# Sparse attention's key projections ahead of head three's gates; the stacking loop ordered head by head

## The chip, the cores and the metric

The kernel runs on one core of a Trainium2 chip. The metric is the device time of one execution in microseconds (us), here the median of three runs. The engines are named as in the profile: PE is TensorE (matmuls and transposes; PEld its weight loads), DVE is VectorE, ACT is ScalarE, POOL is GpSimd, and SP starts the DMAs.

## What is computed

One layer of a decoder trunk over 1024 tokens of width 1024. The normed input is projected once, and the columns of the result go to three groups of heads: a gated linear recurrence (group A, HGRN2, 4 heads of 128), sparse attention with an indexer that picks 256 keys for each query (group B, 4 heads of 64), and attention into 256 memory tokens (group C). Their outputs are joined and projected, and a SwiGLU layer follows. The change touches groups A and B:

```python
def hgrn2_mix(q, f_logit, i, g, lb, out_gain):
    ...
    def step(S, inp):
        qc, kc, vc, gc = inp
        b = jnp.cumsum(gc, axis=2)
        o_inter = jnp.einsum('bhck,bhkv->bhcv', qc * jnp.exp(b), S)
        diff = b[:, :, :, None, :] - b[:, :, None, :, :]
        decay = jnp.exp(jnp.where(causal[:, :, None], diff, -jnp.inf))
        A = jnp.einsum('bhtk,bhtsk,bhsk->bhts', qc, decay, kc)
        o = o_inter + jnp.einsum('bhts,bhsv->bhtv', A, vc)
        ...
        return S, o
    ...
    o = rmsnorm(o, out_gain) * jax.nn.silu(g.astype(f32))

def dsa_mix(q, k, v, iq, ik, iw, q_gain, k_gain):
    ...
    q = rmsnorm(q, q_gain).astype(f32)
    k = rmsnorm(k, k_gain).astype(f32)
    ...
        logits = jnp.einsum('bqhd,bqkhd->bhqk', qb, kg) * (SA_DH ** -0.5)
        logits = jnp.where(valid[:, None], logits, -jnp.inf)
        p = jax.nn.softmax(logits, axis=-1)
        return jnp.einsum('bhqk,bqkhd->bqhd', p, vg)
```

## The kernel before

**Stages.** In the order of time: norm of the input, indexer scores, memory attention, the projections of groups A and B with the recurrences between them, sparse attention (560 to 640 us), the output projection (`wo`), the SwiGLU layer (`ff`, `fo`). The change lies in the projections between 424 us and sparse attention.

**A projection.** `proj` (L186) takes one page of 128 columns of the weights and makes it in two halves `hf` of 512 tokens. A half is 24 matmuls of 128x512: each operand is split into a high and a low part, and three products of them are summed over eight tiles of the model width. The moving operand is the normed input, held in 32 tiles `ht(p, k, hf)` (p the part, k the width tile, hf the half); the result stands in one of two PSUM banks "mm" until `evac` has taken it out. Each page comes by one DMA (`hg_wst`, `sap_wst`) and is split on ACT (L117) and POOL or DVE (L118).

**Group A**, for each head h: `hgrn_proj(h)`, three pages; `hgrn_gates(h)`, sigmoids and products in POOL and ACT; `hgrn_intra(h)`, the products inside a block of 32 tokens in six rounds. A round is `level_products` (32 small matmuls on L518, printed in halves or whole) and then `descend` on the tiles Q, K and F, on DVE (L527), POOL (L528) and DVE (L529), and L543 which takes the round's products out. The next round's matmuls read the tiles that `descend` has just changed, so the rounds wait for one another: PE to DVE and POOL and back. Two wider rounds (L553) follow. `hgrn_state(h)` transposes K (L571), makes the products of keys and values (L578), chains them over the blocks on DVE (L583, L585), makes the output (L594, L596), squares and sums it (L601, L602), takes the inverse root (`narrow_rstd`, L144 to L151, fifteen DVE steps one behind the other) and applies it (L606, L612, L613).

**Group B.** `sparse_queries` projects page 20 and page 21 is projected last of all (`evac_q1`); `sparse_keys` projects pages 18 and 19, and for each half copies the keys into `mt(4)` or `mt(5)` (ACT L734; printed as `sap_m4`, `sap_m5`), squares them (L736), sums the squares (PE L739), takes the inverse root on DVE (L159, L144 to L151), spreads it over rows (L169 on DVE, L172 on PE) and multiplies the keys by it (L744). The storage of `mt(4)` holds the second head's values before. Then the **stacking loop** writes, for each of the four heads and both halves, the queries (`stack`, L253 and L254) and the keys into operand tiles: on ACT the high part (L810), on DVE or POOL the low part (L811). These operand tiles are `ht` tiles again: they lie over the normed input, so a tile of half hf can be written only when the last projection's half hf has read it. The stacked keys `kst` and queries `qst` are what sparse attention's logits read.

**Sparse attention** is a pipeline over 32 items (8 blocks of queries, 4 heads): `sa_logits` (PE L830, DVE L832 adds the mask and takes the maximum, L837 scales it by the query's norm), `sa_exp` (ACT L841), `sa_scale` (POOL L847), `sa_turn` (PE transposes L856, copies L859 on ACT and L861 on DVE), `sa_out` (PE L875). With each item one step of `fillers` is written: first the steps of `hgrn_intra(3)` and `hgrn_state(3)`, then parts of the output projection.

**What sets the order.** Each engine takes its instructions in one fixed order. It is not the order of the program text: a list scheduler places the whole program against a model of the engines' time, and of the instructions that are ready on an engine in that model the one that stands earliest in the text goes first. So moving a call in the text changes which work fills which gap, on all engines.

The calls between the second head's state and sparse attention read (`run` finishes all steps of a generator):

```python
    run(hgrn_state(1))
    hgrn_gates(2)
    run(hgrn_intra(2))
    hgrn_proj(3)
    hgrn_gates(3)
    sparse_keys()
    bisect((7, 4), V, "v")
    run(hgrn_state(2))
```

Heads are numbered from 0 in the code; "head three" in the text is `h = 2`, "head four" is `h = 3`. `bisect` is part of the indexer and finds each query's threshold.

## Time and profile before

| | before |
|---|---|
| median of 3 runs | 1390.32 us (1389.21 to 1392.29) |
| the profiled execution's own time | 1390.27 us |
| its span in the profile | 1388.5 us |
| mean granted clock of PE | 0.973 |
| PE busy | 1302.4 us (94%) |
| DVE busy | 1056.7 us (76%) |
| ACT busy | 692.0 us (50%) |
| POOL busy | 475.1 us (34%) |
| PE's share of the chain that ended last | 59% |
| DVE's share of it | 6% |

The busy times and shares come from the profile's page. The shares are means over stages that are limited in different ways, so they don't say what a change in one stage is worth. The page also cuts the span into 40 slices of 34.7 us and gives each engine's busy share in tenths; in slices 15 and 16 (from 520 to 590 us) PE stands at 5 and 7 (9 in most others), PE's granted clock at 6 and 8, and DVE at 9 and 7. That stretch is the one behind the last projection and ahead of sparse attention.

### The profile page before, as it was taken

The page shows a single profiled execution, that of the slowest core. Times are in us where ns is not written, and L with a number is a line of the kernel's source. Part 1 is how long each engine was busy: PE and PEld are TensorE (multiplying, and loading weights), DVE is VectorE, ACT ScalarE, POOL GpSimd, SP SyncE. Part 2 cuts the span into 40 slices and gives each one's busy share as a digit, 9 for nine tenths or more (in the row PEclk, how much of TensorE's full clock was granted, in tenths as well). Part 3 has the DMA queues.
Part 4 walks back from the last instruction along what each step waited for, and adds up shares of the span by engine and source line. Part 5 has one row for each costly group of instructions (what it writes and reads, how often), then busy time and mean ns, then how long its engine had stood idle before and what let it go on. Part 6 is the DMA issues. An engine that isn't in the chain of part 4 may idle for free.

```text
span 1388.5 us, 22035 instructions
## 1 busy us (share of the span) xinstructions
PE 1302.4 (94%) x8072; PEld 1066.3 (77%) x8072; DVE 1056.7 (76%) x2094; ACT 692.0 (50%) x1369; POOL 475.1 (34%) x395
## 2 busy tenths in 40 slices
...
DMA packets 53244, 122.19 MB, mean 88 GB/s; under 512 B 6032, under 2 KB 6160, under 8 KB 53136
## 3 DMA queue, kind: packets, MB, share of 16 engines
...
## 4 chain that ended last, share of the span: by engine, by line
PE 59%; DVE 6%; POOL 2%; ACT 2%; issue 2%; DMA 1%; ACTq 0%; DVEq 0%; POOLq 0%
PE ff_lg L1093 17%; PE ff_rc L1093 12%; PE fo_mm L1252 4%; PE fo_sm L1252 4%; PE wo_mm L1052 3%; PE fo_lg L1252 2%; PE fo_rc L1252 2%; PE wo_sm L1052 2%; PE sap_mm L186 2%; PE hg_mm L186 2%; PE sat_sm L856 1%; PE sat_lg L830 1%; PE wo_mm L186 1%; PE sat_mm L875 1%; PE sat_rc L875 1%
## 5 line engine op out<-in xcount | busy, mean ns | idle before, releaser
L117 ACT ACTIVATE ff_whi<-ff_x 128x512 fp32r<-128x512 f32 x112 | 70.0, 629 | 125.4 <-PE ff_rc L1093 70.1
L643 ACT ACTIVATE idx_x<-idx_x,packs 128x896 int8<-128x896 f32 (+3 forms) x128 | 105.7, 826 | 41.6 <-DVE packs L638 34.9
L1093 PE MATMUL ff_lg<-wo_h,ff_whi 128*128 128x512 f32 x396 | 104.8, 391 | 2.8 <-ACT wo_h L117 2.8
L186 PE MATMUL hg_mm<-xn_h,hg_whi 128*128 128x512 f32 x384 | 96.9, 395 | 0.0
L1093 PE MATMUL ff_rc<-wo_h,ff_whi 128*128 128x512 f32 x308 | 90.5, 393 | 0.6 <-DVE wo_h L177 0.6
L1093 PE MATMUL ff_lg<-wo_x,ff_whi 128*128 128x512 f32 x308 | 84.9, 404 | 5.3 <-ACT ff_tmp L1100 4.8
L1093 PEld LDWEIGHTS ff_lg<-wo_h,ff_whi 128*128 128x128 f32 x396 | 74.6, 188 | 18.7 <-ACT wo_h L117 3.3
L118 DVE TENSOR_TENSOR ff_wlo<-ff_x,ff_whi 128x512 fp32r<-128x512 f32 x112 | 82.1, 741 | 8.7 <-ACT ff_whi L117 4.0
L186 PEld LDWEIGHTS hg_mm<-xn_h,hg_whi 128*128 128x128 f32 x384 | 70.5, 188 | 14.5 <-issue 0.7
L118 POOL TENSOR_TENSOR hg_wlo<-hg_wst,hg_whi 128x512 fp32r<-128x512 f32 x32 | 43.0, 1356 | 104.9 <-ACT hg_whi L117 79.4
L1093 PEld LDWEIGHTS ff_lg<-wo_x,ff_whi 128*128 128x128 f32 x308 | 57.6, 192 | 24.0 <-ACT ff_whi L117 7.3
L646 DVE TENSOR_SCALAR_CACHE_REDUCE idx_x<-idx_x,packs 128x1024 int8<-128x1024 f32 x64 | 68.7, 1074 | 0.9
L1093 PEld LDWEIGHTS ff_rc<-wo_h,ff_whi 128*128 128x128 f32 x308 | 58.6, 190 | 13.6 <-DVE wo_h L177 1.4
L1093 PE MATMUL ff_rc<-wo_x,ff_whi 128*128 128x512 f32 x220 | 64.3, 389 | 0.0
L1030 POOL TENSOR_TENSOR ff_x<-ff_wst 128x512 f32<-128x512 f32 x7 | 13.4, 1911 | 134.6 <-PE wo_sm L1052 71.3
L528 POOL TENSOR_TENSOR hg_x<-hg_x,hg_x 128x256 f32<-128x256 f32 x56 | 49.4, 898 | 29.0 <-PE hg_rc L518 18.7
L1093 PE MATMUL ff_lg<-wo_h,ff_wlo 128*128 128x512 f32 x198 | 55.8, 390 | 0.0
L388 DVE SCALAR_TENSOR_TENSOR idx_x<-idx_tmp,packs,idx_x 128x512 f32<-128x512 f32 (+2 forms) x70 | 46.1, 710 | 12.2 <-ACT idx_tmp L383 11.9
L118 DVE TENSOR_TENSOR fo_wlo<-fo_tmp,fo_whi 128x512 fp32r<-128x512 f32 x33 | 33.2, 1006 | 27.0 <-ACT fo_whi L117 27.0
L186 PE MATMUL hg_mm<-xn_h,hg_wlo 128*128 128x512 f32 x192 | 50.9, 397 | 0.0
L1093 PEld LDWEIGHTS ff_rc<-wo_x,ff_whi 128*128 128x128 f32 x220 | 41.3, 188 | 8.6
L118 DVE TENSOR_TENSOR fo_wlo<-fo_h,fo_whi 128x512 fp32r<-128x512 f32 x31 | 33.5, 1081 | 18.1 <-ACT fo_whi L117 18.0
...
## 6 DMA issues: line engine op xcount, KB each, us to landing
...
```

The costliest lines, as they stand in the source:

```text
L117: S.activation(hi, src, AF.Copy)
L118: (eng or V).tensor_sub(lo, src, hi.bitcast(F32))
L186: T.matmul(ps[:M, :], w(pw, k), h[p][k][hf], start=i == 0, stop=i == len(order) - 1)
L388: V.scalar_tensor_tensor(sc[b][:, c0:c1], rl[:, :c1 - c0], iww[:, b, h:h + 1], sc[b][:, c0:c1], op0=ALU.mult, op1=ALU.add)
L528: G.tensor_mul(Kv[:, :, 0, :], Kv[:, :, 0, :], fr.to_broadcast([128, n, w]))
L643: S.activation(waste[S][:, :nk], sc[b], AF.Sign, bias=nf[:, j:j + 1], accum_out=ct[:, j:j + 1])
L646: eng.tensor_scalar(waste[eng][:, :nk], sc[b], fl[:, j:j + 1], None, op0=ALU.is_ge, op1=ALU.add, accum_out=ct[:, j:j + 1])
L830: T.matmul(lg[:, :c1 - c0], qst[h][b // 4][:, bs(b % 4)], kst[h][p][c][:, :c1 - c0], start=p == 0, stop=p == 1)
L875: T.matmul(po[ROWS[j], 0:128], sv[kb // 4][:, kb % 4, 128 * m + 64 * j:128 * m + 64 * j + 64], PTs[j][:, kb, :], start=kb == 0, stop=kb == ...
L1052: mm = T.matmul(ps, lhs, rhs, start=i == 0, stop=i == len(steps) - 1)
L1093: mm = T.matmul(ps, w[pw][:, bs(k)], HB[u][k][p], start=first and i == 0, stop=i == 11, skip_group_check=True)
L1252: T.matmul(banks[m], w[i][pw][:, bs(m)], b[i][p], start=first and i == 0 and n == 0, stop=i == NP - 1 and n == 2, skip_group_check=True)
```

## The change

The call of `sparse_keys()` moves from behind head four's gates to a place ahead of head three's gates, so that the key projections come ahead of head three's rounds and of head four's projections. The stacking loop runs over the heads outside and the halves inside; before, it ran over the halves outside and the heads inside. The operations in both loops are the same ones, and each engine issues as many of them as before.

```diff
@@ -775,11 +775,11 @@
     run(hgrn_intra(1))
     hgrn_v(1)
     run(hgrn_state(1))
+    sparse_keys()
     hgrn_gates(2)
     run(hgrn_intra(2))
     hgrn_proj(3)
     hgrn_gates(3)
-    sparse_keys()
     bisect((7, 4), V, "v")
     run(hgrn_state(2))
     bisect((6, 5, 3, 2), S, "s")
@@ -796,19 +796,18 @@
     ph[0] = "sap"
     proj(page(21), 128, H, evac_q1)
     kst = [[[None, None], [None, None]] for _ in range(4)]
-    for hf in range(2):
-        for m in range(2):
-            for j in range(2):
-                h = 2 * m + j
-                if m == 0:
-                    qst[h][hf] = ht(0, h, hf)
-                    stack(qst[h][hf].unsqueeze(1), sqr[0][:, hs(hf)], 0, ROWS[j], V_SAQ)
-                for p in range(2):
-                    kst[h][p][hf] = ht(1 - p, h + 4 * p, hf)
-                src = kr[m][ROWS[j], hs(hf)]
-                for o, e in ((ROWS[j], V), (ROWS[1 - j], G)):
-                    S.activation(kst[h][0][hf][o], src, AF.Copy)
-                    e.tensor_sub(kst[h][1][hf][o], src, kst[h][0][hf][ROWS[j]].bitcast(F32))
+    for h in range(4):
+        m, j = divmod(h, 2)
+        for hf in range(2):
+            if m == 0:
+                qst[h][hf] = ht(0, h, hf)
+                stack(qst[h][hf].unsqueeze(1), sqr[0][:, hs(hf)], 0, ROWS[j], V_SAQ)
+            for p in range(2):
+                kst[h][p][hf] = ht(1 - p, h + 4 * p, hf)
+            src = kr[m][ROWS[j], hs(hf)]
+            for o, e in ((ROWS[j], V), (ROWS[1 - j], G)):
+                S.activation(kst[h][0][hf][o], src, AF.Copy)
+                e.tensor_sub(kst[h][1][hf][o], src, kst[h][0][hf][ROWS[j]].bitcast(F32))
     q_scale()
 
     ph[0] = "sat"
```

From the first row of PE's order to 424 us, and again from 660 us on, the order of every engine is the same in both kernels (line numbers from L810 on are one lower after the change). Between them it shows the change at three places.

On PE, head three's `hgrn_intra` (L518 on `hg_x0_567` and `hg_x1_568`; L186 on `hg_mm` is head four's projection, on `sap_mm` the keys' projection; `xn_h` is the normed input). Before, around its third round:

```order
L186 MATMUL hg_mm665_4622<-xn_h39_167,hg_wlo661_4589 128x512
L186 MATMUL hg_mm665_4622<-xn_h41_171,hg_wlo661_4589 128x512
L518 MATMUL hg_rc634_4249<-hg_x0_567_3371,hg_x1_568_3372 32x32 x32
L186 MATMUL hg_mm665_4622<-xn_h43_175,hg_wlo663_4593 128x512
L186 MATMUL hg_mm665_4622<-xn_h45_179,hg_wlo663_4593 128x512
L186 MATMUL hg_mm665_4622<-xn_h47_183,hg_wlo663_4593 128x512
L186 MATMUL hg_mm665_4622<-xn_h49_187,hg_wlo663_4593 128x512
L186 MATMUL sap_mm674_4677<-xn_h19_127,sap_whi670_4669 128x512
```

and now, all of its six rounds:

```order
L186 MATMUL sap_mm664_4358<-xn_h49_187,sap_wlo656_4295 128x512
L518 MATMUL hg_rc672_4435<-hg_x0_567_3371,hg_x1_568_3372 32x32 x32
L518 MATMUL hg_rc673_4471<-hg_x0_567_3371,hg_x1_568_3372 32x32 x32
L518 MATMUL hg_rc674_4511<-hg_x0_567_3371,hg_x1_568_3372 32x32 x32
L518 MATMUL hg_rc675_4551<-hg_x0_567_3371,hg_x1_568_3372 32x32 x32
L518 MATMUL hg_rc676_4591<-hg_x0_567_3371,hg_x1_568_3372 32x32 x16
L172 MATMUL sap_sm650_4280<-packs_79,sap_tmp651_4281 128x128 x4
L739 MATMUL sap_sm659_4326<-packs_79,sap_tmp658_4324 128x2 x4
L518 MATMUL hg_rc676_4591<-hg_x0_567_3371,hg_x1_568_3372 32x32 x16
L518 MATMUL hg_rc677_4631<-hg_x0_567_3371,hg_x1_568_3372 32x32 x16
L186 MATMUL hg_mm690_4734<-xn_h19_127,hg_whi686_4726 128x512
```

Before, twelve to twenty-four projection matmuls (of head four's pages, then of the keys) stood between one round and the next; now four and a half rounds stand in a row, two rows of the key normalisation stand between the halves of the fifth round, and head four's projection (`hg_mm690`) begins behind the sixth.

On POOL, the subtractions of the stacking loop (`m4` holds the keys of the first two heads, `m5` of the others). Before:

```order
L811 TENSOR_TENSOR sap_h738_5580<-sap_m4_667_4665,sap_h737_5579 64x512
L811 TENSOR_TENSOR sap_h741_5589<-sap_m4_667_4665,sap_h740_5588 64x512
L811 TENSOR_TENSOR sap_h743_5595<-sap_m5_668_4666,sap_h742_5594 64x512
L811 TENSOR_TENSOR sap_h745_5601<-sap_m5_668_4666,sap_h744_5600 64x512
L811 TENSOR_TENSOR sap_h748_5610<-sap_m4_667_4665,sap_h747_5609 64x512
L811 TENSOR_TENSOR sap_h751_5619<-sap_m4_667_4665,sap_h750_5618 64x512
L811 TENSOR_TENSOR sap_h753_5625<-sap_m5_668_4666,sap_h752_5624 64x512
L811 TENSOR_TENSOR sap_h755_5631<-sap_m5_668_4666,sap_h754_5630 64x512
```

and now:

```order
L810 TENSOR_TENSOR sap_h738_5580<-sap_m4_631_4156,sap_h737_5579 64x512
L810 TENSOR_TENSOR sap_h744_5598<-sap_m4_631_4156,sap_h743_5597 64x512
L810 TENSOR_TENSOR sap_h749_5613<-sap_m5_632_4157,sap_h748_5612 64x512
L810 TENSOR_TENSOR sap_h753_5625<-sap_m5_632_4157,sap_h752_5624 64x512
L810 TENSOR_TENSOR sap_h741_5589<-sap_m4_631_4156,sap_h740_5588 64x512
L810 TENSOR_TENSOR sap_h747_5607<-sap_m4_631_4156,sap_h746_5606 64x512
L810 TENSOR_TENSOR sap_h751_5619<-sap_m5_632_4157,sap_h750_5618 64x512
L810 TENSOR_TENSOR sap_h755_5631<-sap_m5_632_4157,sap_h754_5630 64x512
```

The four rows of the first half still stand ahead of the four of the second half: the tiles that they write have another numbering, their places have not moved.

On DVE, the first instructions that write the stacked keys, behind the first half of the last projection. Before:

```order
L811 TENSOR_TENSOR sap_h738_5580<-sap_m4_667_4665,sap_h737_5579 64x512
L118 TENSOR_TENSOR wo_h873_6435<-mat_m6_364_1630,wo_h872_6434 128x512
L811 TENSOR_TENSOR sap_h741_5589<-sap_m4_667_4665,sap_h740_5588 64x512
L118 TENSOR_TENSOR wo_h878_6445<-mat_m7_365_1631,wo_h877_6444 128x512
L254 SCALAR_TENSOR_TENSOR sap_h736_5576<-sap_x12_525_2982,packs_79,sap_h736_5576 64x512
L254 SCALAR_TENSOR_TENSOR sap_h739_5585<-sap_x12_525_2982,packs_79,sap_h739_5585 64x512
L602 TENSOR_REDUCE hg_so714_5136<-hg_x2_713_5135 128x4
L744 SCALAR_TENSOR_TENSOR sap_m5_668_4666<-sap_m5_668_4666,packs_79,sap_sm698_4859 128x512
L159 TENSOR_TENSOR sap_rk703_4900<-sap_sm702_4895,packs_79 128x8
L144 TENSOR_SCALAR sap_abx704_4902<-sap_rk703_4900 128x8
```

and now:

```order
L583 COPY hg_x1_710_5118<-hg_rc711_5119 128x128
L585 SCALAR_TENSOR_TENSOR hg_x1_710_5118<-hg_x1_710_5118,hg_tot680_4718,hg_rc711_5119 128x128 x2
L810 TENSOR_TENSOR sap_h738_5580<-sap_m4_631_4156,sap_h737_5579 64x512
L810 TENSOR_TENSOR sap_h744_5598<-sap_m4_631_4156,sap_h743_5597 64x512
L585 SCALAR_TENSOR_TENSOR hg_x1_710_5118<-hg_x1_710_5118,hg_tot680_4718,hg_rc711_5119 128x128
L810 TENSOR_TENSOR sap_h749_5613<-sap_m5_632_4157,sap_h748_5612 64x512
L810 TENSOR_TENSOR sap_h753_5625<-sap_m5_632_4157,sap_h752_5624 64x512
L118 TENSOR_TENSOR wo_h873_6435<-mat_m6_364_1630,wo_h872_6434 128x512
L118 TENSOR_TENSOR wo_h878_6445<-mat_m7_365_1631,wo_h877_6444 128x512
L585 SCALAR_TENSOR_TENSOR hg_x1_710_5118<-hg_x1_710_5118,hg_tot680_4718,hg_rc712_5128 128x128
L254 SCALAR_TENSOR_TENSOR sap_h736_5576<-sap_x12_525_2982,packs_79,sap_h736_5576 64x512
```

Before, the rows of the last key normalisation (L744, L159, L144 and on) and a sum of head three's output squares (L602) came soon behind the first two subtractions. Now the key normalisations lie ahead of this place, four subtractions stand here together, and steps of head three's state (L583, L585) stand between them.

## Rows read from the trace of the kernel before

**Rows 1.** Stretches: start:end, length, busy PE, PEld, DVE, ACT, POOL, PE clock, DMA, GB/s.

```profile
459.00:480.00 21.00, 21.00 (x312) 16.64 (x314) 14.67 (x20) 5.70 (x10) 14.48 (x14) 1.00 0.11 38
...
520.00:540.00 20.00, 10.88 (x36) 8.61 (x36) 19.40 (x55) 12.64 (x21) 5.65 (x5) 0.61 0.24 79
540.00:560.00 20.00, 11.21 (x413) 8.93 (x412) 19.20 (x60) 2.48 (x5) 9.25 (x10) 0.59 0.01 2
...
580.00:640.00 60.00, 59.77 (x465) 48.19 (x463) 44.18 (x166) 38.92 (x89) 15.64 (x20) 1.00 0.11 36
...
544.80:558.80 14.00, 6.93 (x385) 5.63 (x384) 13.39 (x40) 1.28 (x3) 8.40 (x9) 0.62 0.01 2
557.50:585.30 27.80, 26.09 (x265) 21.86 (x267) 21.08 (x78) 19.59 (x37) 14.38 (x17) 0.86 0.01 2
```

**Rows 2.** PE's timeline (start, duration), head three's round and what follows it.

```profile
462.88 0.76 PE L518 MATMUL hg_rc<-hg_x,hg_x 128*32 128x32 f32 x64
463.57 3.90 PE L186 MATMUL hg_mm<-xn_h,hg_whi 128*128 128x512 f32 x16
```

**Rows 3.** PE's timeline, head four's rounds; in brackets the wait before.

```profile
549.29 0.66 PE L518 MATMUL hg_rc<-hg_x,hg_x 128*32 128x32 f32 x32 [0.52 <-DVE hg_x L527]
...
551.35 0.66 PE L518 MATMUL hg_rc<-hg_x,hg_x 128*32 128x32 f32 x32 [1.40 <-DVE hg_x L527]
```

**Rows 4.** PE's timeline, last projection to first transposes of attention.

```profile
517.95 1.98 PE L186 MATMUL sap_mm<-xn_h,sap_wlo 128*128 128x512 f32 x8
528.50 2.05 PE L172 MATMUL sap_sm<-packs,sap_tmp 128*128 128x128 f32 x8 [8.58 <-DVE sap_tmp L169]
...
560.51 1.97 PE L856 MATMUL sat_sm<-packs,sat_x 128*128 128x128 f32 x8 [0.85 <-POOL sat_x L847]
```

**Rows 5.** PE's timeline, matmuls of the key normalisation.

```profile
500.26 1.06 PE L172 MATMUL sap_sm<-packs,sap_tmp 128*128 128x128 f32 x8
501.15 0.95 PE L739 MATMUL sap_sm<-packs,sap_tmp 128*128 128x2 f32 x8
```

**Rows 6.** DVE's timeline, normalisation steps, subtractions, first logits, ninth copy L861.

```profile
502.96 0.17 DVE L149 SCALAR_TENSOR_TENSOR sap_abx<-sap_abx 128x8 f32<-128x8 f32 x1
...
508.73 0.68 DVE L811 TENSOR_TENSOR sap_h<-sap_m,sap_h 64x512 fp32r<-64x512 f32 x1 [0.92 <-PE sap_mm L186]
...
519.10 1.67 DVE L811 TENSOR_TENSOR sap_h<-sap_m,sap_h 64x512 fp32r<-64x512 f32 x1
...
534.94 0.69 DVE L832 CUSTOM_DVE_ANT_0 sat_x<-sat_lg,idx_x 128x512 f32<-128x512 f32 x1
...
585.28 0.54 DVE L861 COPY sat_x<-sat_sm 128x384 f32<-128x384 f32 x1
```

**Rows 7.** POOL's timeline, four subtractions of the stacking loop.

```profile
517.06 6.19 POOL L811 TENSOR_TENSOR sap_h<-sap_m,sap_h 64x512 fp32r<-64x512 f32 x4 [4.23 <-ACT sap_h L810]
```

**Rows 8.** ACT's timeline, first exponential of sparse attention.

```profile
557.52 1.24 ACT L841 ACTIVATE sat_x<-sat_x,sat_mz,packs 128x1024 f32<-128x1024 f32 x1 [20.82 <-DVE sat_mz L837]
```

**Rows 9.** DVE's groups, 508.7 to 534.9: count, then busy us, mean ns, idle before.

```profile
L811 DVE TENSOR_TENSOR sap_h<-sap_m,sap_h 64x512 fp32r<-64x512 f32 x6 | 6.1, 1009 | 1.0 <-PE sap_mm L186 0.9
L149 DVE SCALAR_TENSOR_TENSOR sap_abx<-sap_abx 128x8 f32<-128x8 f32 x4 | 1.7, 437 | 0.0
...
L744 DVE SCALAR_TENSOR_TENSOR sap_m<-sap_m,packs,sap_sm 128x512 f32<-128x512 f32 x2 | 1.5, 741 | 0.0
```

**Rows 10.** DVE's groups, 534.9 to 557.5.

```profile
L527 DVE TENSOR_TENSOR hg_x<-hg_x,hg_x 128x256 f32<-128x256 f32 x7 | 2.9, 412 | 0.0
...
L613 DVE SCALAR_TENSOR_TENSOR hg_m<-hg_rc,packs,hg_m 128x512 f32<-128x512 f32 x2 | 1.5, 738 | 0.0
```

**Rows 11.** PE's groups, 557.5 to 585.3.

```profile
L578 PE MATMUL hg_rc<-hg_x,hg_x 128*128 128x128 f32 x14 | 1.7, 275 | 0.0
...
L571 PE MATMUL hg_rc<-packs,hg_x 128*128 128x128 f32 x8 | 1.3, 279 | 0.0
```

**Rows 12.** The chain that ended last, 424 to 760 us: the wait for a weight page.

```profile
641.58 3.81 DMA wo_wst<-woa
```

## The prediction

> **What bounds the kernel now.** I read first the engines' busy time by stretch [rows 1], to see where TensorE is not the bound. It works without a break in 459 to 480 and almost so in 580 to 640. Between 520 and 560 it does not: 10.9 and 11.2 us busy of 20 each, at a mean granted clock of 0.61 and 0.59 of full speed, so at the lower of its two levels (1.2 of 2.4 GHz) for most of it. There VectorE is full, 19.4 and 19.2 us of 20. So before 520 and after 580 a matmul more costs its time; in the hole a VectorE instruction more does.
>
> Then the two ways in which the rounds L518 of `hgrn_intra` stand. Head three's run under projections: a round of 0.76 us and 3.90 us of projection matmuls right behind it, no idle time [rows 2]. Head four's stand alone: each half round waits 0.5 to 1.4 us for VectorE's L527 [rows 3], and the stretch from the first round to the sixth, 14.0 us long, has TensorE busy 6.9 us at clock 0.62 [rows 1].
>
> Then the hole. TensorE's last projection matmuls start at 517.95 and end near 519.9; it then waits 8.58 us for VectorE's `sap_tmp` (the last of the four key normalisations), and the first transposes of attention stand at 560.51 [rows 4]. VectorE's first key subtraction is at 508.73 and the first logits are reduced at 534.94 [rows 6]; the first exponential is at 557.52, ScalarE having waited 20.82 us for the row maximum scaled by the queries' norm [rows 8].
>
> Outside 424 to 660 the order is the same in both kernels, so what the change does to the end of attention near 640 goes to the end. The wait for a weight page there (3.81 us, [rows 12]) moves along: its loads stand behind the same last attention item as before.
>
> **Keys first.** The 96 key matmuls take the place of the first 96 of head four's, in the same slots, same shapes, same page loads in the SP queue: nothing until head three's rounds begin. ScalarE copies the keys into `m4`, which the second head's values hold till L594 is through, so its queue waits there; behind it stands L601, the squares of head three's output. I cost that at nothing: the sums of those squares (L602) now stand behind the last projection, where VectorE comes to them late in any case.
>
> **The rounds lose their cover.** In the new TensorE order four and a half rounds of head three stand in a row, then L172 and L739, the other half, and only then head four's first projection. Why TensorE can't take that projection sooner: it is an in-order queue. Nearest row for uncovered rounds: head four's, 14.0 us for six. Of these, TensorE's own work at full speed is six times 0.76 [rows 2], 4.6 us, so 9.4 us are lost there. In the new place the span is longer (two pairs L172 and L739 of 1.06 + 0.95 us [rows 5], and 14 projection matmuls of 0.23 us, 3.2 us, stand between the halves). If all of that lay inside the waits, 9.4 - 7.2 = 2.2 us were lost; but the first four rounds have nothing between them (two thirds of the 9.4, 6.3), and behind the last the next L172 waits for a normalisation of fifteen dependent VectorE steps of 0.2 us (one stands in [rows 6]), which here share VectorE with the rounds: 1 to 4 us. Bounds 7 and 13, taken 10.
>
> **Moved work.** Two L172 and one L739 (3.1 us with [rows 5]) stood behind the first half of the last projection and now stand ahead. So that first half ends 3 + 10 = 13 us later, and VectorE's first key subtraction moves from 508.7 to 521.7.
>
> **From there to the first logits, VectorE.** Before: 26.2 us without a gap. Out: the last key normalisation, L744 twice, nine steps of the other chain (`hg_abx`) and one L602; by the rows of that stretch 11.1 us, of which [rows 9] has the two largest (1.7 + 1.5; L150, L151 and small ones are the rest). In: two L811 of 1.0, four L585 of 0.35, one L404, 3.6 us. But much of what goes is waiting: L149 took 0.437 us in the mean [rows 9] where the same step takes 0.17 undisturbed [rows 6]. L811 on VectorE takes 0.68 us alone and 1.67 while GpSimd does its own four of 6.19 us [rows 6, 7]. Summed over the stretch this waiting is 3.5 us in rows that go and 2 in rows that stay, for six GpSimd subtractions, 0.9 each. It hangs on GpSimd and does not go with the rows; all eight subtractions now fall here: 3.5 stays and 1.8 is added. Sum 26.2 - 11.1 + 3.6 + 3.5 + 1.8 = 24.0. Lower bound, waiting gone: 18.7. First logits at 521.7 + 24.0 = 545.7, 10.8 later than before. On waiting I go by these rows. The Trainium skill ("SBUF — State Buffer", Who interferes with whom) says that a VectorE instruction with two SBUF inputs and a GpSimd one that reads SBUF lock each other out for the whole instruction. By that rule the eight would cost VectorE up to their whole eight times 1.55 = 12.4 us (6.19 for four) instead of about 7, and the result would be some 5 us worse (an estimate); the trace agrees in part: VectorE's 1.67 beside GpSimd is longer than its own 0.68, but shorter than 0.68 + 1.55.
>
> **From the first logits to the first exponential.** Before 22.6 us. Out: head four's rounds (seven L527, 2.9; L529, L536, L537, L543) and L613 (1.5), two L811 and L404, together 11.6 (two of them in [rows 10]). In: twelve steps of `hg_abx` and an L602, 2.7. That gives 13.7; if the chain steps that GpSimd's L528 stretched come back to 0.17, 3.8 less, 9.9. GpSimd has only its tail of subtractions there, so nearer the lower: 11. Exponential at 556.7, 0.8 earlier than before. This is where the hole's gain shows: 13 us late at the start, level again here.
>
> **Attention with rounds in it.** Head four's rounds now stand between attention items. Before, from the first exponential to the ninth copy L861 (585.28, [rows 6]), VectorE was busy 21.1 of 27.8 us [rows 1]. In: four L527, the large L529, L536, L537, three L543, L613, 8.2 us; out: L583, six L585, an L118 and two small ones, 3.6. Then 25.7 plus waiting of GpSimd rows fills the 27.8; bounds 28 and 31, taken 29: 585.7, 0.4 late. By that point head four's L571, L578 and half of L594 and L596, done before, are not: 1.1 + 1.55 + 1.56 = 4.2 us at full clock (the first two in [rows 11], with the low clock in them). From here TensorE is full to 640 [rows 1], so they are added whole. Sum: +0.4 + 4.2 = 4.6 us.
>
> **Head by head.** The loop's new order changes little: the second half of every head's tiles lies over input tiles that the last projection's second half still reads, so the built GpSimd order takes all first halves, then all second halves, as before. Costed at nothing; if it were wrong, head one's second half would come one subtraction later, 1.5 us.
>
> The profiled execution took 1390.27 us (span 1388.5), as the median 1390.32. 1390.3 + 4.6 = 1394.9, so **1395**.
>
> **Rivals.** *The hole closes for good.* If the waiting for GpSimd goes with the chain (18.7 and 9.9), the exponential is at 521.7 + 18.7 + 9.9 = 550.3, 7.2 early; with 28 us for the next stretch and the 4.2 of late work, the end is 2.8 early, and with the rounds at 8 instead of 10 some 4.5: **1386**. For it: the full 40 us of hole. It decides when the first logits are reduced before about 541. Against it: GpSimd's eight subtractions are all still there.
> *It cancels.* Rounds at 7, all else as forecast: 1392; or only one of the two VectorE stretches at its lower end: 1389 to 1391. **1391**.
> *The clock stays low.* The two waits in the uncovered rounds and the mixed stretch both look like 544 to 559, at 0.62. If the lower level holds through the projections behind the rounds and through half of the attention stretch, about 6 us of matmuls count double: **1401**. Against it: between 480 and 500 nothing would keep TensorE waiting. The Trainium skill ("TensorE: Matmul & The Clock Gate", HAM oscillation) says that bursts with waits between them are throttled anew each time; the trace agrees where the rounds stand alone.
>
> **Chances.** Forecast (1393.1 to 1399) 0.40, the clock 0.12, cancelling (1387.5 to 1393.1) 0.25, the hole closed (below) 0.23. What a measurement here can tell from no change is about 0.2%, 2.8 us. Slower 0.52, same 0.25, faster 0.23. The range leaves some 0.1 on each side: 1385 to 1402. The likeliest case alone: 1393 to 1399.
>
> **What would show it.** Right, step by step: idle TensorE between the first and the sixth round of head three, 7 to 13 us where there was none; the last projection's end 8 us or so later than 519.9; VectorE without gaps behind it and the first logits' reduction near 546; the first exponential within 3 us of 557.5; VectorE above 90% to about 586; the end of attention at 643 to 646. Wrong: rounds with less than 5 us of idle time; an exponential before 551; TensorE with gaps after 600; or a change behind 660, where I expect none.

## The result, and the profile after

The changed kernel takes **1398.7 us** (median of 4 runs, 1396.6 to 1400.9) against 1391.3 (4 runs, 1389.2 to 1392.9): 1.0055 of the time before, with a 95% interval of 1.0039 to 1.0071. It is slower by 7.4 us, where 1395 was forecast with a range of 1385 to 1402. The profiled execution took 1399.64 us (span 1397.9), 9.4 more than the one of before, so the times read below add up to some 2 us more than the medians differ by. Lines from L811 of before on are one lower in the new kernel (L811 is L810, L861 is L860).

The copy of before at 585.28 [rows 6] is the seventh of its row behind the first exponential, not the ninth as the text ahead has it. Its counterpart below is the seventh. "The hole" is, as there, the stretch between the last projection and sparse attention.

Stretches of after, with the columns of [rows 1]: start:end, length, busy PE, PEld, DVE, ACT, POOL, PE clock, DMA, GB/s.

```profile
459.00:480.00 21.00, 14.92 (x383) 12.57 (x383) 19.02 (x62) 1.57 (x3) 8.82 (x10) 0.60 0.08 28
480.00:500.00 20.00, 20.00 (x166) 16.27 (x165) 11.57 (x36) 5.11 (x10) 7.83 (x10) 1.00 0.06 17
500.00:520.00 20.00, 20.00 (x94) 16.62 (x94) 3.66 (x6) 7.26 (x13) 7.99 (x8) 1.00 0.11 33
```

TensorE, full in 459 to 480 before, is now idle for 6 of these 21 us, at a mean granted clock of 0.60 of full speed where it was 1.00. And VectorE, which before was busy for most of 500 to 520, has next to nothing to do there (3.66 us): the key normalisations that it did under the last projection are past, and what replaces them waits for TensorE. Before, the same two stretches ahead of the hole read:

```profile
480.00:500.00 20.00, 20.00 (x244) 16.53 (x232) 16.73 (x58) 6.61 (x14) 9.77 (x13) 1.00 0.06 18
500.00:520.00 20.00, 19.93 (x128) 17.57 (x126) 16.58 (x43) 10.81 (x19) 6.48 (x4) 1.00 0.09 27
```

From 459 to 520 VectorE was busy for 48.0 us before and is for 34.3 now (with [rows 1]). Of the 13.7 us between them 8.4 come back later: from 520 to the start of the output projection it is busy for 108.3 us, where it was 99.9. The rest is time that its instructions no longer take: from 424 on it has the same work (521 and 522 instructions in the trace) and is busy for 168.6 us with it, where it was 175.9 (rows from 424 below).

TensorE's timeline of after, head three's rounds (start, duration; in brackets the wait before), to be held against [rows 2]:

```profile
459.91 0.76 PE L518 MATMUL hg_rc<-hg_x,hg_x 128*32 128x32 f32 x64
462.11 0.46 PE L518 MATMUL hg_rc<-hg_x,hg_x 128*32 128x32 f32 x32 [1.43 <-DVE hg_x L536]
...
467.15 0.66 PE L518 MATMUL hg_rc<-hg_x,hg_x 128*32 128x32 f32 x32 [1.39 <-DVE hg_x L527]
468.58 0.65 PE L518 MATMUL hg_rc<-hg_x,hg_x 128*32 128x32 f32 x32 [0.77 <-DVE hg_x L527]
469.90 0.65 PE L518 MATMUL hg_rc<-hg_x,hg_x 128*32 128x32 f32 x32 [0.67 <-DVE hg_x L527]
471.03 2.04 PE L172 MATMUL sap_sm<-packs,sap_tmp 128*128 128x128 f32 x8 [0.48 <-DVE sap_tmp L169]
...
475.51 5.59 PE L186 MATMUL hg_mm<-xn_h,hg_whi 128*128 128x512 f32 x14
```

From the second round on the half rounds wait for VectorE, as only head four's did before [rows 3]; L172 takes 2.04 us where it took 1.06 [rows 5]. Head four's projection begins only at 475.51, and the lower clock outlasts the rounds: from 463 to 480 the granted clock is 0.50 throughout (the lower of its two levels, 1.2 of 2.4 GHz), although TensorE has no gap from 475.51 on, and the first 14 matmuls of the projection take 5.59 us, where 16 took 3.90 [rows 2].

Then the marks that the prediction set, from the timelines of VectorE, ScalarE and TensorE of after: first key subtraction, first logits reduced, first exponential, seventh copy, first matmul of the output projection's last part (L1051, L1052 in before; some earlier parts run among the attention items).

```profile
524.15 2.39 DVE L810 TENSOR_TENSOR sap_h<-sap_m,sap_h 64x512 fp32r<-64x512 f32 x2
...
547.18 0.69 DVE L831 CUSTOM_DVE_ANT_0 sat_x<-sat_lg,idx_x 128x512 f32<-128x512 f32 x1
...
588.48 0.55 DVE L860 COPY sat_x<-sat_sm 128x384 f32<-128x384 f32 x1
```

```profile
557.43 1.24 ACT L840 ACTIVATE sat_x<-sat_x,sat_mz,packs 128x1024 f32<-128x1024 f32 x1 [10.05 <-DVE sat_mz L836]
```

```profile
656.18 0.98 PE L1051 MATMUL wo_mm<-wo_x,wo_whi 128*128 128x512 f32 x3 [0.80 <-ACT wo_whi L117]
```

They stood at 508.73, 534.94, 585.28 [rows 6], 557.52 [rows 8] and, the last, at 645.99. Kernels with almost the same order differ by some 1.5 us at such a mark in their profiles (after and keys_only, before and heads_only below), so a smaller difference of a mark shows nothing. So after is 15.4 us late at the first key subtraction, level at the first exponential, 3.2 late at the seventh copy and 10.2 late at the output projection. The prediction looked for the gain where it indeed shows, at the exponential; the question is why it is gone 100 us further on. The three stretches between the marks, of after and then of before:

```profile
524.15:557.43 33.28, 21.06 (x93) 17.45 (x92) 32.50 (x84) 17.77 (x30) 13.11 (x8) 0.71 0.13 48
557.43:588.48 31.05, 27.08 (x583) 21.64 (x583) 29.31 (x85) 17.12 (x32) 20.50 (x23) 0.87 0.01 3
588.48:656.18 67.70, 63.96 (x486) 49.66 (x482) 45.61 (x181) 42.79 (x104) 18.04 (x26) 1.00 0.15 48
```

```profile
508.73:557.52 48.79, 31.99 (x473) 26.23 (x471) 47.25 (x121) 19.56 (x32) 19.68 (x16) 0.70 0.10 34
557.52:585.28 27.76, 26.07 (x264) 21.84 (x266) 21.04 (x78) 19.57 (x37) 14.38 (x17) 0.86 0.01 2
585.28:645.99 60.71, 58.33 (x447) 45.78 (x443) 42.59 (x166) 40.04 (x99) 17.55 (x24) 1.00 0.17 54
```

The stretch to the exponential is 15.5 us shorter, but TensorE does 10.9 us less in it: 93 matmuls instead of 473. The difference is nearly all head four's rounds and states. The rounds come behind the exponential (583 matmuls against 264), and head four's state, which lay beside them, comes behind the seventh copy, where TensorE has 5.6 us more to do. The groups of TensorE in that last stretch of after (count, then busy us, mean ns):

```profile
L594 PE MATMUL hg_rc<-hg_x,hg_x 128*128 128x128 f32 x16 | 2.9, 275 | 0.0
L596 PE MATMUL hg_rc<-hg_x,hg_x 128*128 128x128 f32 x14 | 2.7, 275 | 0.0
...
L578 PE MATMUL hg_rc<-hg_x,hg_x 128*128 128x128 f32 x14 | 2.0, 282 | 0.0
L571 PE MATMUL hg_rc<-packs,hg_x 128*128 128x128 f32 x8 | 1.3, 278 | 0.0
```

Before, L571 and L578 were done by then, and L594 and L596 had 8 matmuls each left.

From 424 us, where the two executions are still within 0.1 us of each other, to the first key subtraction and to the output projection; of before, then of after:

```profile
424.00:508.73 84.73, 82.89 (x837) 68.90 (x837) 65.02 (x161) 25.36 (x47) 45.08 (x43) 1.00 0.11 34
424.00:645.99 221.99, 199.28 (x2014) 162.75 (x2013) 175.89 (x521) 104.53 (x213) 96.69 (x100) 0.92 0.11 35
...
424.00:524.15 100.15, 91.95 (x862) 77.16 (x861) 61.20 (x178) 27.63 (x50) 44.27 (x45) 0.91 0.09 29
424.00:656.18 232.18, 204.06 (x2014) 165.90 (x2012) 168.62 (x522) 105.31 (x213) 95.92 (x101) 0.90 0.10 34
```

Up to the output projection TensorE carries out the same 2014 matmuls in both. Of the 10.2 us, 5.4 are more idle time (28.1 against 22.7) and 4.8 are the same matmuls taking longer.

### The profile page after: what moved, and what is told of

The parts are those of the page before. It is cut to its first block, busy times and chain, and to the rows that moved or that the text cites. A ratio compares the mean times of both kernels' runs of the same rounds, so it can differ in the third digit from the quotient of the medians.

```text
span 1397.9 us, 22029 instructions
## 1 busy us (share of the span) xinstructions
PE 1308.4 (94%) x8072; PEld 1071.5 (77%) x8072; DVE 1051.0 (75%) x2094; ACT 692.6 (50%) x1369; POOL 474.0 (34%) x395
## 4 chain that ended last, share of the span: by engine, by line
PE 58%; DVE 6%; issue 2%; POOL 2%; ACT 2%; DMA 1%; ACTq 0%; DVEq 0%; POOLq 0%
PE ff_lg L1092 17%; PE ff_rc L1092 12%; PE fo_mm L1251 4%; PE fo_sm L1251 4%; PE wo_mm L1051 3%; PE fo_rc L1251 3%; PE fo_lg L1251 3%; PE hg_mm L186 3%; PE wo_sm L1051 2%; PE sap_mm L186 1%; PE wo_mm L186 1%; PE sat_rc L874 1%; PE sat_lg L829 1%; POOL hg_x L528 1%; PE sat_sm L855 1%
## 5 line engine op out<-in xcount | busy, mean ns | idle before, releaser
L186 PE MATMUL hg_mm<-xn_h,hg_whi 128*128 128x512 f32 x384 | 98.8, 401 | 0.0
L118 DVE TENSOR_TENSOR ff_wlo<-ff_x,ff_whi 128x512 fp32r<-128x512 f32 x112 | 82.2, 743 | 9.2 <-ACT ff_whi L117 4.0
L186 PEld LDWEIGHTS hg_mm<-xn_h,hg_whi 128*128 128x128 f32 x384 | 72.2, 192 | 15.2 <-issue 0.7
L118 POOL TENSOR_TENSOR hg_wlo<-hg_wst,hg_whi 128x512 fp32r<-128x512 f32 x32 | 41.8, 1316 | 120.8 <-ACT hg_whi L117 80.7
L1092 PEld LDWEIGHTS ff_lg<-wo_x,ff_whi 128*128 128x128 f32 x308 | 57.7, 192 | 24.1 <-ACT ff_whi L117 7.4
L1029 POOL TENSOR_TENSOR ff_x<-ff_wst 128x512 f32<-128x512 f32 x7 | 13.4, 1910 | 137.6 <-PE wo_sm L1051 74.3
L528 POOL TENSOR_TENSOR hg_x<-hg_x,hg_x 128x256 f32<-128x256 f32 x56 | 49.1, 890 | 27.9 <-PE hg_rc L518 15.5
L388 DVE SCALAR_TENSOR_TENSOR idx_x<-idx_tmp,packs,idx_x 128x512 f32<-128x512 f32 (+2 forms) x70 | 46.1, 713 | 12.3 <-ACT idx_tmp L383 12.0
L118 DVE TENSOR_TENSOR fo_wlo<-fo_tmp,fo_whi 128x512 fp32r<-128x512 f32 x33 | 33.2, 1007 | 27.0 <-ACT fo_whi L117 27.0
L846 POOL TENSOR_SCALAR sat_x<-sat_x,sat_mz 128x1024 f32<-128x1024 f32 (+7 forms) x32 | 25.9, 811 | 75.2 <-DVE sat_mz L845 37.2
L186 PE MATMUL hg_mm<-xn_h,hg_wlo 128*128 128x512 f32 x192 | 50.6, 396 | 0.0
```

Of the source, the lines that this page charges most:

```text
L118: (eng or V).tensor_sub(lo, src, hi.bitcast(F32))
L186: T.matmul(ps[:M, :], w(pw, k), h[p][k][hf], start=i == 0, stop=i == len(order) - 1)
L388: V.scalar_tensor_tensor(sc[b][:, c0:c1], rl[:, :c1 - c0], iww[:, b, h:h + 1], sc[b][:, c0:c1], op0=ALU.mult, op1=ALU.add)
L528: G.tensor_mul(Kv[:, :, 0, :], Kv[:, :, 0, :], fr.to_broadcast([128, n, w]))
L846: G.tensor_scalar(P[:, :nk], P[:, :nk], mx[:, 2:3], 1.0, op0=ALU.mult, op1=ALU.mult)
L1092: mm = T.matmul(ps, w[pw][:, bs(k)], HB[u][k][p], start=first and i == 0, stop=i == 11, skip_group_check=True)
```

## The experiments

The theory as it stood after this reading: (1) the keys' move alone makes the loss, by baring head three's rounds; (2) the rounds are bare because the bank that head four's projection needs is given back late; (3) what the hole gives back is small because the waiting of VectorE's rows belongs to GpSimd's subtractions and stays. The rivals: the loop's new order costs something; the loss is the place of head four's rounds among the attention items; or the GpSimd scaling of the attention items, now beside rounds, holds it up.

The 39 us that one of the expectations names for the stretch behind the first exponential run to the ninth copy of after, at 596.25; the table goes by the seventh.

All runs in one table: median, ratio to the kernel before on the same chip with its 95% interval, the time of the first key subtraction in the profile, and the three stretches as above (to the first exponential, to the seventh copy, to the output projection), in us.

| run | median | ratio | first key subtraction | stretches | sum |
|---|---|---|---|---|---|
| before | 1391.3 | 1 | 508.7 | 48.8, 27.8, 60.7 | 137.3 |
| after | 1398.7 | 1.0055 [1.0039, 1.0071] | 524.2 | 33.3, 31.1, 67.7 | 132.0 |
| keys_only | 1400.4 | 1.0069 [1.0046, 1.0093] | 525.5 | 33.2, 31.1, 67.6 | 131.9 |
| heads_only | 1390.4 | 0.9991 [0.9976, 1.0006] | 507.2 | 48.7, 27.6, 60.4 | 136.6 |
| square_from_copy | 1396.3 | 1.0038 [1.0024, 1.0053] | 514.4 | 37.8, 31.3, 66.6 | 135.6 |
| before_square | 1389.8 | 0.999 [0.9977, 1.0002] | 508.8 | 48.4, 28.9, 59.6 | 136.9 |
| sub_dve | 1400.6 | 1.0064 [1.0045, 1.0082] | 523.4 | 36.1, 31.9, 66.4 | 134.3 |
| scale_act | 1398.4 | 1.0046 [1.0029, 1.0062] | 522.7 | 33.2, 30.5, 66.0 | 129.7 |
| square_mm | 1398.9 | 1.0057 [1.0037, 1.0078] | 512.7 | 45.0, 30.7, 66.1 | 141.8 |
| after_state | 1401.1 | 1.0058 [1.0035, 1.0081] | 529.2 | 39.5, 27.3, 60.5 | 127.3 |
| before_state | 1409.2 | 1.0118 [1.0090, 1.0146] | 524.9 | 47.6, 32.2, 57.7 | 137.4 |
| before_sub_dve | 1392.4 | 0.9999 [0.9985, 1.0014] | 508.4 | 43.4, 27.7, 66.5 | 137.6 |
| before_no_chain | 1393.4 | 1.0009 [0.9994, 1.0024] | 508.7 | 47.8, 31.6, 58.7 | 138.1 |

**One part alone.** keys_only moves the keys and keeps the old stacking loop:

```diff
     run(hgrn_state(1))
+    sparse_keys()
     hgrn_gates(2)
     run(hgrn_intra(2))
     hgrn_proj(3)
     hgrn_gates(3)
-    sparse_keys()
```

> Only the keys' projection is moved; the stacking loop stands as before the change. Theory (the keys' move does it all, the loop's order nothing): the ratio of the changed kernel, 1.0055, so 1398 to 1400 us, and the same rows: first key subtraction on VectorE near 524, first exponential near 557, first matmul of the output projection near 656. Rival (the loop's order costs or gives some of it, because GpSimd's subtractions stand in another numbering): more than 2 us away from 1398.7 in either direction.

heads_only does the other half, the loop, with the keys where they were:

```diff
-    for hf in range(2):
-        for m in range(2):
-            for j in range(2):
-                h = 2 * m + j
...
+    for h in range(4):
+        m, j = divmod(h, 2)
+        for hf in range(2):
...
```

> Only the stacking loop is changed to head by head; the keys' projection stays where it was. Theory (the input tiles under the operand tiles allow no other order): the time of the kernel before, 1391 within 1.5 us, first exponential at 557.5. Rival (the loop's order is a part of the loss): 1393 to 1395.

keys_only has the loss (1400.4, 0.4 above the range that was expected), heads_only has none: the stretches of the one are those of after to 0.2 us, those of the other those of before to 0.4. The first rival fell.

**The bank.** Each half of a key projection leaves its PSUM bank in two readings by ScalarE, the copy L734 and the square L736. In after the copies and squares of the last halves stand so in ScalarE's queue (its timeline), and the fourth half's projection so in TensorE's:

```profile
451.28 0.60 ACT L734 ACTIVATE sap_m<-sap_mm 128x512 f32<-128x512 f32 x1 [5.80 <-PE sap_mm L186]
...
460.02 0.60 ACT L734 ACTIVATE sap_m<-sap_mm 128x512 f32<-128x512 f32 x1 [3.00 <-PE sap_mm L186]
460.51 1.08 ACT L736 ACTIVATE sap_tmp<-sap_mm 128x512 f32<-128x512 f32 x2
```

```profile
452.42 3.93 PE L186 MATMUL sap_mm<-xn_h,sap_whi 128*128 128x512 f32 x16 [0.30 <-ACT sap_tmp L736]
```

The fourth half's projection waits for a square (the second half's), as that has its bank. The third half is copied at 451.28, but its square runs only at 460.51, behind the copy of the fourth: so both banks of the pair are held until the keys are through, and the order built for TensorE has head four's projection behind the rounds. square_from_copy takes that reason away; the square reads the copy, and the bank is free after one reading:

```diff
                 S.activation(o, ps, AF.Copy)
                 sq = tmp()
-                S.activation(sq, ps, AF.Square)
+                S.activation(sq, o, AF.Square)
```

> The changed kernel with one edit in the keys' evacuation: ScalarE squares the keys from their copy and no longer from the PSUM bank, so a projection's bank is free as soon as it has been copied. Theory one (head three's rounds lost their cover because head four's first projection could not have a bank: one of the two was held by a square that stood late in ScalarE's queue): each of the six rounds again has some 19 or 20 projection matmuls behind it, TensorE has no idle time in 460 to 480, the last projection's first half ends some 12 us sooner (first key subtraction 510 to 513 instead of 524), the stretches behind it keep their lengths (23, 10 and 39 us), the output projection starts at 643 to 646: 1385 to 1389 us, level with the kernel before or up to 5 us faster. Rival (VectorE's sum of work and head four's rounds inside attention set the end, wherever the projections end): the exponential comes earlier but the stretch behind it gets longer by the same amount, 1395 to 1399 us.

TensorE's timeline of square_from_copy at the same place, ScalarE's with the third half's square, and the stretch 459 to 480:

```profile
458.50 3.12 PE L186 MATMUL hg_mm<-xn_h,hg_whi 128*128 128x512 f32 x13
...
463.23 0.76 PE L518 MATMUL hg_rc<-hg_x,hg_x 128*32 128x32 f32 x64
463.93 0.97 PE L186 MATMUL hg_mm<-xn_h,hg_whi 128*128 128x512 f32 x3
...
468.71 0.76 PE L518 MATMUL hg_rc<-hg_x,hg_x 128*32 128x32 f32 x64
```

```profile
468.04 0.62 ACT L736 ACTIVATE sap_tmp<-sap_m 128x512 f32<-128x512 f32 x1
```

```profile
459.00:480.00 21.00, 21.00 (x290) 17.63 (x289) 15.52 (x42) 3.87 (x7) 8.53 (x8) 1.00 0.13 43
```

Head four's projection begins at 458.50, ahead of the third half's square. The rounds are covered again, TensorE has no idle time, the granted clock is 1.00, and the first key subtraction comes 9.8 us sooner than in after. So the bank is what bared them. But the output projection comes only 6.2 us sooner in the profile, and the median is 2.4 us below that of after and 4.1 below that of keys_only, which ran on the same chip. The time that was expected (1385 to 1389) was missed: with the rounds covered the kernel is still slower than before (1.0038), so the bared rounds are a third to a half of the loss and not, as theory (1) had it, all of it. The rival named the time (1395 to 1399), but not for its reason: the stretch behind the exponential doesn't get longer (97.8 us, 98.8 in after). What the rest hangs on no run shows apart; in the profile the first key subtraction is 5.6 us later than in before, 3.1 of which the moved normalisation matmuls would make (an estimate, from [rows 5]), and head four's late work is still behind the exponential (31.3 and 66.6 us). The stretch to the exponential is 4.5 us longer than in after, and VectorE's groups in it (of square_from_copy; idle time before, and for what) say why:

```profile
L810 DVE TENSOR_TENSOR sap_h<-sap_m,sap_h 64x512 fp32r<-64x512 f32 x8 | 8.6, 1078 | 4.5 <-PE sap_mm L186 4.3
...
L831 DVE CUSTOM_DVE_ANT_0 sat_x<-sat_lg,idx_x 128x512 f32<-128x512 f32 x6 | 4.0, 685 | 1.7 <-PE hg_rc L596 1.7
```

VectorE begins with the subtractions sooner, but the input tiles that the next ones write over are still read by the last projection, and it waits 4.3 us for that; in after it never does (0.2). The control is the same edit in the kernel before:

> The same edit (squares from the copy) in the kernel before, keys where they were. It is the control for the run with that edit in the changed kernel. Theory one: there the rounds had their cover anyway, so nothing is gained ahead of 520; 1389 to 1392 us. Rival (the edit is worth something by itself, because a bank comes free sooner in any order): 1383 to 1387, and then its share has to be taken off the other run's gain.

It changes nothing that can be measured there, so the edit itself shows no price.

**GpSimd's subtractions.** sub_dve puts all sixteen key subtractions of after on VectorE, before_sub_dve does so in the kernel before:

```diff
-            for o, e in ((ROWS[j], V), (ROWS[1 - j], G)):
+            for o, e in ((ROWS[j], V), (ROWS[1 - j], V)):
```

> The changed kernel with all sixteen key subtractions of the stacking loop on VectorE, none on GpSimd. VectorE gets eight instructions of 0.68 us more, 5.5 us. Theory (VectorE's rows behind the last projection are long because GpSimd's eight subtractions, 13.65 us without a gap, stand beside them): the four subtractions, two L118 and two L254 that took 11.9 us there take 5.6, so the stretch from the first key subtraction to the first logits stays at 22 to 23 us, and the whole at 1397 to 1400. Rival (their length has another cause, or VectorE's count of instructions is what matters): these rows keep their length, the stretch takes 28 us or more, 1403 to 1405 us.

> The kernel before with all sixteen key subtractions on VectorE, none on GpSimd. Theory (a VectorE row that stands beside a GpSimd subtraction waits for it, whichever row it is, so the waiting belongs to GpSimd's instructions): between the first key subtraction and the first logits every step of the normalisation chain (L149, L150, L151, up to 1.25 us there) takes 0.17 us, L811 0.69 and L118 0.69; 6.4 us of waiting go, eight subtractions of 0.69 come, and the stretch of 26.2 us becomes 25 to 26. 1390 to 1393 us. Rival (the long chain steps wait for something of their own, so they are a price of the chain): they stay at 0.4 us in the mean, the stretch takes 30 us or more, 1395 to 1398 us.

VectorE's groups from the first key subtraction to the first logits (count, then busy us, mean ns, idle before), of after:

```profile
L810 DVE TENSOR_TENSOR sap_h<-sap_m,sap_h 64x512 fp32r<-64x512 f32 x8 | 8.2, 1022 | 0.2
L118 DVE TENSOR_TENSOR wo_h<-mat_m,wo_h 128x512 fp32r<-128x512 f32 x4 | 4.6, 1193 | 0.0
L254 DVE SCALAR_TENSOR_TENSOR sap_h<-sap_x,packs,sap_h 64x512 fp32r<-64x512 f32 x4 | 4.5, 1131 | 0.1
```

and of sub_dve:

```profile
L810 DVE TENSOR_TENSOR sap_h<-sap_m,sap_h 64x512 fp32r<-64x512 f32 x16 | 11.0, 685 | 0.2
...
L254 DVE SCALAR_TENSOR_TENSOR sap_h<-sap_x,packs,sap_h 64x512 fp32r<-64x512 f32 x4 | 3.0, 748 | 0.1
L118 DVE TENSOR_TENSOR wo_h<-mat_m,wo_h 128x512 fp32r<-128x512 f32 x4 | 2.6, 688 | 0.0
...
L831 DVE CUSTOM_DVE_ANT_0 sat_x<-sat_lg,idx_x 128x512 f32<-128x512 f32 x1 | 0.7, 692 | 2.6 <-PE hg_rc L596 2.6
```

Without GpSimd beside them all rows go back to their undisturbed price: 0.69 for L810 and L118, 0.75 for L254. The eight GpSimd subtractions of after (13.65 us in one block from 524.14) cost VectorE 2.7 + 2.0 + 1.5 = 6.2 us by these groups; on VectorE they take 8 x 0.685 = 5.5. That is no gain, and sub_dve is where after is (1400.6, the expected 1400 just missed; its first logits come 25.8 us behind the first subtraction, not 22 to 23, of which it waits 2.6 for TensorE). In before_sub_dve the chain steps L149 and L150 take 0.16 us where L149 took 0.437 [rows 9], and the exponential comes 5.75 us sooner. Yet this, too, brings nothing. Its timelines of ScalarE and TensorE:

```profile
551.77 1.24 ACT L841 ACTIVATE sat_x<-sat_x,sat_mz,packs 128x1024 f32<-128x1024 f32 x1 [10.65 <-DVE sat_mz L837]
```

```profile
645.97 0.96 PE L1052 MATMUL wo_mm<-wo_x,wo_whi 128*128 128x512 f32 x3 [0.51 <-ACT wo_whi L117]
```

The output projection starts at 645.97, in before at 645.99. In this order L578, four of the L571 and all of L594 and L596 stand behind the seventh copy, much as in after, and the last stretch is 66.5 us instead of 60.7. A first exponential that is early because head four's work has been passed over is early on credit: the work is done later, where TensorE is full. (The time was met, 1390 to 1393; the first logits came 19.2 us behind the first subtraction, not 25 to 26, in an order that the edit had changed.)

before_no_chain takes away the rows instead of the engine beside them: the last key half's root is left out.

```diff
+                if m == 1 and hf == 1:
+                    rk = last[0]
+                else:
...
```

> The kernel before without the last key half's own inverse root: the sums of its squares and the fifteen dependent VectorE steps are left out, and it is multiplied by the root of the half before. So one chain of those that the moved keys take out of the stretch is gone, and nothing else is moved. In the trace of before these rows took 5.4 us between the first key subtraction and the first logits, of which 2.7 us at their undisturbed 0.17 us. Theory (waiting stays, since it belongs to GpSimd's subtractions; other rows take it over): the stretch shrinks from 26.2 to 23 to 24.5 us, the first exponential comes 1.5 to 3.5 us sooner, 1388 to 1391 us. Rival (rows leave with the waiting that they show): 21 us or less, the exponential 5 us sooner, 1385 to 1387.

VectorE's groups of before_no_chain between the same marks:

```profile
L815 DVE TENSOR_TENSOR sap_h<-sap_m,sap_h 64x512 fp32r<-64x512 f32 x8 | 7.8, 976 | 0.7 <-PE sap_mm L186 0.6
...
L150 DVE TENSOR_TENSOR hg_abx<-hg_abx 128x8 f32<-128x8 f32 x4 | 1.6, 403 | 0.1
L149 DVE SCALAR_TENSOR_TENSOR hg_abx<-hg_abx 128x8 f32<-128x8 f32 x4 | 1.6, 402 | 0.1
...
L146 DVE TENSOR_SCALAR hg_abx<-hg_abx 128x8 int32<-128x8 int32 x1 | 1.1, 1115 | 0.0
```

With the long steps of the key chain gone, others are long: a step L146 takes 1.1 us and L149 and L150 0.40 in the mean, where 0.16 is the undisturbed price. By the groups of both runs the waiting is 6.3 us, where it was 6.4 in before. The rows left, the waiting stayed. The forecast of the time failed all the same: the order changed, all eight GpSimd subtractions fall ahead of the first logits, which come 28.4 us behind the first subtraction (23 to 24.5 were expected), and the median is that of before (1388 to 1391 were expected).

**GpSimd's scaling of the attention items.** scale_act gives the first eight items' scaling by the row sum to ScalarE:

```diff
-        G.tensor_scalar(P[:, :nk], P[:, :nk], mx[:, 2:3], 1.0, op0=ALU.mult, op1=ALU.mult)
+        if t["i"] < 8:
+            S.activation(P[:, :nk], P[:, :nk], AF.Copy, scale=mx[:, 2:3])
+        else:
+            G.tensor_scalar(P[:, :nk], P[:, :nk], mx[:, 2:3], 1.0, op0=ALU.mult, op1=ALU.mult)
```

> The changed kernel with the scaling of the first eight attention items on ScalarE and no longer on GpSimd. Theory (in 557 to 597, where head four's rounds stand among the items, each item and each round wait for GpSimd in turn, and VectorE's L527, L529 and L836 are longer beside it): VectorE's rows there get shorter by 2 to 4 us and a round waits less, the exponential stays at 557, the output projection starts at 652 to 654, 1394 to 1397 us. Rival (VectorE's and TensorE's own work fills that stretch, or ScalarE's exponentials wait for the scalings now): the stretch from the first exponential to the output projection stays at 98 us or gets longer, 1398 to 1403.

The stretches behind the exponential are 2.3 us shorter in the profile, the median is level with that of after (1398.4 and 1398.7; 1394 to 1397 were expected). At most some 2 us of the loss are this; the rival fell as the main cause.

**The place of head four's rounds.** Two ways to bring them ahead of attention again. square_mm adds to square_from_copy that head four's rounds go to the other pair of banks, so that they need not wait for head three's output:

```diff
-            rc = bank("rc")
+            rc = bank("mm" if h == 3 else "rc")
```

> The changed kernel with squares from the copy (as in the run before), and head four's rounds write to the two PSUM banks of the projections, which are free by then, and no longer to the two that hold head three's output until it is normalised. So its rounds can start before that. Position theory (rounds among the attention items cost some 9 us, because an item and a round wait for each other): rounds start near 540, the exponential moves to 552 to 557, the stretch from it to the output projection shrinks from 98 to 90 us, 1389 to 1393 us. Sum theory (VectorE's work from the first key subtraction on sets the end, wherever the rounds stand in it): exponential later, stretch shorter by the same amount, 1394 to 1398 us.

The first rounds do stand ahead of attention (539.95 to 550), but the rest waits for the same banks among the attention items' outputs, and VectorE is idle for 7.5 us of 560 to 580. Its median is above that of square_from_copy (1.0057 against 1.0038, the intervals overlap) and above what either theory named (1389 to 1393, 1394 to 1398), and since it trades one conflict of banks for another it doesn't decide the question. after_state takes another way, by the order alone: head three's state ahead of head four's projection.

```diff
     run(hgrn_intra(2))
+    run(hgrn_state(2))
     hgrn_proj(3)
...
-    run(hgrn_state(2))
```

> The changed kernel with head three's state (transposes, state chain, output, normalisation) written ahead of head four's projections. In TensorE's order its steps then stand between those projections, the bare rounds of head three stay as they are, and head four's rounds stand ahead of the first attention transposes again, as in the kernel before. Theory (head three's output comes so late in the changed kernel that head four's rounds fall among the attention items, and VectorE, idle for 22 of the 26 us under head four's projections, gets its work only behind them): VectorE does the state chain and the normalisation in 497 to 523, the first exponential comes at 552 to 558 with head four's rounds ahead of it, the stretch from it to the output projection shrinks from 98 to 88 or 90 us, 1386 to 1392 us. Rival (the stretch of 98 us is VectorE's sum and not the rounds' place, and the rounds now delay the exponential by as much): 1394 to 1400 us.

Now the rounds stand ahead of attention as in before, and the last two stretches are those of before (27.3 and 60.5 us). But the exponential comes 11.3 us later than in after, at 568.73, and the output projection starts at 656.55, against 656.18. The 10.9 us that the attention stretches win are paid ahead of them: 6.2 in the hole, where head four's rounds now stand, and 5.1 ahead of the first key subtraction, where TensorE now has head three's output to make (L594, L596 and L612 take 6.7 us more there). The ratio is that of after (1.0058), and neither theory's time (1386 to 1392, 1394 to 1400) was met. So this way of moving the rounds ahead gains nothing; as head three's state moves with them, the run doesn't show the rounds' place by itself. before_state is the same line moved in the kernel before, ahead of the keys:

> The kernel before, keys where they were, with head three's state written ahead of the keys' projection. Head four's rounds then begin under the keys' last and the query projections instead of in the bare stretch 544 to 559; head three's last two steps and its state lose their cover. Theory (the hole behind the last projection is VectorE's sum, and what is done ahead of it shortens it): 8 to 14 us of VectorE's work leave the hole, the exponential comes 6 to 12 us sooner, less some 6 us of uncovered steps of head three: 1383 to 1390 us. Rival (what is uncovered at head three's last steps costs as much as the hole gives back): 1390 to 1396.

```profile
507.87 1.97 PE L612 MATMUL hg_rc<-packs,hg_x 128*128 128x128 f32 x8 [5.23 <-DVE hg_x L606]
```

```profile
500.00:520.00 20.00, 14.77 (x115) 13.31 (x114) 14.80 (x65) 3.71 (x7) 0.00 (x0) 0.91 0.04 13
```

It is the slowest of all (1.0118), against what was expected of it. Here another dependent chain is bared: ahead of the last projection TensorE waits 5.2 us at one place for the normalisation of head three's output (L606). From 424 to the first key subtraction, which comes at 524.9, as late as in after, TensorE has 6.9 us more of idle time than in before and 9.3 more of work, 7.6 of them head three's output. Its three stretches then sum to 137.4, as in before, so that all 16 us of delay go to the end. Why the stretches don't get shorter, though this work has left them, wasn't followed.

## Why the prediction was right, and where its terms were off

The sign and the place of the loss were right, and the time lies in the range, which was wide (17 us, down to below the kernel before). The size was not right in each part: all three costs came out larger than taken, 7.3 us together, and the hole's gain was 1.7 larger too, which hides a part of it. The terms, against what the profile of after shows:

| step | forecast | measured |
|---|---|---|
| first key subtraction later | +13 | +15.4 |
| to the first logits | -2.2 | -3.2 |
| to the first exponential | -11.6 | -12.3 |
| to the seventh copy | +1.2 | +3.3 |
| to the output projection | +4.2 | +7.0 |
| sum | +4.6 | +10.2 |

**The rounds' cover: the mechanism right, the size 2.3 us short.** From 459.91 to 475.51 TensorE is busy 9.5 of 15.6 us; at full speed the five and a half rounds and the two normalisation steps in it take 5.5 times 0.76 and 2.0 us, 6.2, so 9.4 us are lost there. The prediction priced the 14 projection matmuls behind them at full speed, 3.2 us; still at the lower clock, they took 5.59. The whole shows from 424 on: the first key subtraction is 15.4 us late, 3.1 of it are the moved matmuls, and 12.3 remain where 10 was taken (bounds 7 and 13). About half of that is idle time (8.2 us against 1.8), the other half the lower clock. So the sign that was named, 7 to 13 us of idle time, was missed from below (6.1 from 459.91 to 475.51). In square_from_copy, where the rounds are covered, the start comes 9.8 us sooner. The reason was only half right: TensorE keeps to the order that was built (it idles among the rounds, although both squares are through by 461.6 and head four's projection stands behind them), which explains why the order isn't mended at run time, but not why it was built so. That was the bank.

**Moved work: right.** The sum had two L172 and one L739 more ahead of the first key subtraction. By TensorE's groups from 424 to that mark there are just these (32 matmuls of L172 against 16, 32 of L739 against 24, eight to a row); the projection matmuls are 263 in both.

**The hole: right, a little better than forecast.** First logits 3.2 us sooner after the start, first exponential at 557.43 where 556.7 was forecast. GpSimd's price was taken a little too high: the sum has about 7 us of waiting there (3.5 kept, 2 in rows that stay, 1.8 added), and after shows 6.2. It also read before's waiting too low: by the groups of that stretch it was 6.4, not 5.5, as the L118 there wait too (0.926 us for 0.69). So the waiting hardly changed, though all eight GpSimd subtractions now fall there. The Trainium skill ("SBUF — State Buffer", Who interferes with whom) has VectorE and GpSimd lock each other out for the whole instruction; taken at its whole price that is the prediction's estimate of up to 12.4 us, and the 6.2 measured here are half of it. That the waiting hangs on GpSimd and not on the rows that show it was an assumption, and before_no_chain, sub_dve and before_sub_dve show it from three sides.

**Attention with rounds in it: short.** I counted four L527 more ahead of the copy at 585.28; its counterpart has thirteen in front of it behind the exponential where there were seven, so six more, and each takes 0.53 us in the mean instead of 0.43. VectorE is busy for 29.3 us where 25.7 were counted, and the stretch grew by 3.3 us instead of 1.2. What makes the L527 longer isn't shown; with the scalings on ScalarE (scale_act) they take 0.58, so GpSimd's scalings don't.

**The late matmuls: short.** The mechanism was right, TensorE's work of head four falls into a stretch that TensorE bounds. Of L594 and L596 fourteen matmuls more are left over, beside L571, L578 and L553: by busy time 5.6 us more instead of 4.2. And TensorE, which had 2.4 us of gaps in this stretch, now has 3.7: the 1.4 more lie between 615 and 620, where it waits for VectorE, for masked logits (L831) and for head four's normalisation (L606, L613). Gaps behind 600 were named as a sign against the forecast; they are there (18.53 busy of 20 in 600 to 620, before 19.77), and they are 1.4 of the 2.8 us missed.

**The rivals.** *The hole closes for good* didn't happen: the exponential is level, not 7 us early. *It cancels* neither. *The clock stays low* named 1401, near to the measured time, and happened in part: the lower clock held through the first 14 projection matmuls behind the rounds, 2.2 us (5.59 instead of 3.4 at the rate of [rows 2]), not the 6 it named; from 480 to 520 and from 580 on the granted clock is 1.00, and in attention with rounds it is what it was (0.87 and 0.86). **Head by head** costs nothing (heads_only). Behind 660 the order is the same, as forecast, and from the mark of the output projection to the end the execution takes 0.8 us less.

What stays open: what makes the part of the loss that is left when the rounds are covered; and why the median of square_from_copy gains 2.4 us on after where its profiled execution gains 4.1 and its output projection starts 6.2 sooner. A version faster than the kernel before was not found (the three that stand lowest, before_square, heads_only and before_sub_dve, have 1 in their intervals).
